# Second block: the token's rms scale moves from the operand of projection and MLP to the units behind them

## The chip, the cores and the metric

One core of one Trainium2 chip. The metric is the device time of one execution in microseconds, the median of the runs. One further execution was taken with the hardware profiler; the trace is from that one.

## The reference, cut to what matters

Two blocks one after the other on x, 256 tokens of 2048 numbers: an RWKV block with a modulated norm and a convolutional FFN (`first_block`), then the block that the change is about. `rmsnorm` divides each token by its root mean square and multiplies each feature by a weight.

```python
def rmsnorm(x, gain):
    xf = x.astype(jnp.float32)
    y = xf * lax.rsqrt(jnp.mean(xf * xf, axis=-1, keepdims=True) + EPS)
    return (y * gain.astype(jnp.float32)).astype(x.dtype)
...
        h = rmsnorm(x, mix_pre_gain[layer])
        proj = jnp.einsum('bsd,de->bse', h, w_in[layer])
        q_a, k_a, v_a, q_r, f_r, i_r, g_r = jnp.split(proj, SPLITS, axis=-1)
        attn = sliding_window_attention(q_a, k_a, v_a, attn_sinks[layer])
        attn = rmsnorm(attn, attn_out_gain[layer])
        rnn = hgrn2_chunkwise(q_r, f_r, i_r, g_r, lb_all[layer], rnn_norm_gain[layer])
        mixed = jnp.einsum('bse,ed->bsd', jnp.concatenate([attn, rnn], axis=-1), w_out[layer])
        x = x + rmsnorm(mixed, mix_post_gain[layer])
        h = rmsnorm(x, mlp_pre_gain[layer])
        u = jax.nn.relu(jnp.einsum('bsd,df->bsf', h, w_up[layer]))
        y = jnp.einsum('bsf,fd->bsd', u * u, w_down[layer])
        x = x + rmsnorm(y, mlp_post_gain[layer])
```

## The kernel before, in words

Every product is fp32 in three passes: each operand is split into a rounded half `hi` and a remainder `lo`, and hi x hi, hi x lo and lo x hi are added up in a PSUM bank. Weights come by DMA in pieces of 128 x 1024 (`wdma`), and `wsplit` splits them (L183 on ScalarE, L184 on VectorE) into three rotating buffers ahead of their use. The kernel fixes the order of the instructions itself: each engine's queue is the order in which the code issues them.

The stages follow each other: RWKV mixer, its FFN (`ffn`), second block's mixer (`mix`), MLP (`mlp`). `feat` and `feat_p` make a unit: 128 output features of all 256 tokens, 48 matmuls of 256 columns with the operand `hl` (features on partitions, hi and lo). A unit's result is evacuated from its bank some matmuls into the next unit (`deferred`, `flush`). The mixer has 42 units (`mix_evac`), and between their matmuls `mpump` issues the steps of three streams: attention heads and two alternating HGRN heads, due after so many slots. The MLP has 64 units (`ev`, L1813 and L1814).

A stage ends in a token-major product (`tok_all`, or `mix_out` and what follows it): eight banks `acc[tb, cb]`, tokens 0 to 127 (tb 0) or 128 to 255 (tb 1) by 512 columns. `tail` holds back the last weight pieces, so that tb 0 is finished first and then tb 1 in 12 steps, with the end of tb 0 issued between them. In `tail`:

- `col`: the sum of squares of a column block (ScalarE, L325) and its product z with the gain row G (VectorE, L372);
- `row`: the token's first rsqrt (sum L376, Ln L298, Exp L299), then four additions x += z * r (L380), each followed on ScalarE by the squares of the new x;
- `diag`: from the new squares the second rsqrt, multiplied onto the identity: a diagonal matrix `dg` (L391, L393);
- `xp`: 16 matmuls of x against `dg` (L403) turn the tokens' rows into features and scale each token at once; `prep_evac` multiplies each by its norm weight (L337, ScalarE, into `hb`), and `hilo` makes the two halves from `hb` (L285, L288, VectorE). `_attn_out` uses the same `prep_evac` in the middle of the mixer (L319).

`hook` splits weight pieces of the next stage at fixed steps. Two tails feed the second block and have no shift: that at the end of `ffn` (called from `tok_all`, steps of 3 pieces by 4 column blocks) and that at the end of `mix` (6 pieces by 2 column blocks). The tail of the RWKV mixer has a shift, that of the MLP has no next stage.

Of the kernel before, what the change touches and what calls it, by code (L numbers as in the profile page):

```python
# [19 lines left out]
D = 2048  # L20
# [77 lines left out]
class Kern:  # L98
# [228 lines left out]
    def prep_evac(self, wk, tb, hl, gain, shift):  # L327

        nc = self.nc
        t0 = slice(tb * 128, tb * 128 + 128)  # L330

        def evac(j, pt):
            h = wk.tile([128, 4, 128], F32, tag="hb", bufs=2, name="hb")
            for i in range(4):
                kc = j * 4 + i
                if shift is None:
                    nc.scalar.activation(out=h[:, i, :], in_=pt[:, i, :], func=AF.Copy, scale=gain(kc))  # L337
                else:
                    nc.scalar.activation(out=h[:, i, :], in_=pt[:, i, :], func=AF.Identity, scale=gain(kc),
                                         bias=shift(kc))  # L340
            self.hilo(hl[:, 0, j * 4:j * 4 + 4, t0], hl[:, 1, j * 4:j * 4 + 4, t0], h[:], True)
        return evac
# [13 lines left out]
    def tail(self, wk, acc, mm, cbs, G, z, gain, shift, banks, hook, hl=None):  # L356
# [4 lines left out]
        last = gain is None  # L361
        if not last and hl is None:
# [11 lines left out]
        def row(tb):  # L374
# [3 lines left out]
            for cb in range(4):  # L378
                w = slice(cb * 512, cb * 512 + 512)
                nc.vector.scalar_tensor_tensor(out=xt[:, tb, w], in0=z(tb, cb), scalar=r, in1=xt[:, tb, w],  # L380
                                               op0=ALU.mult, op1=ALU.add)
                if last:
                    nc.sync.dma_start(out=self.A["out"][tb * 128:tb * 128 + 128, w], in_=xt[:, tb, w])
                else:
                    self.ssq_(wk, xt[:, tb, w], ss[tb][:, 4 + cb:5 + cb])

        def diag(tb):
            if last:
                return
# [5 lines left out]
        def xp(tb):  # L395
            if last:
                return
            evac = self.prep_evac(wk, tb, hl, gain, shift)
            for j in range(4):
                pt = self.bank(banks[tb][j], (128, 4, 128), "xp")  # L400
                for i in range(4):
                    o = (j * 4 + i) * 128
                    nc.tensor.matmul(pt[:, i, :], lhsT=xt[:, tb, o:o + 128], rhs=dg[tb][:], start=True, stop=True)  # L403
                evac(j, pt)
                yield
# [8 lines left out]
        row(0)  # L414
        steps = [(cb, n) for cb in cbs for n in range(self.ntail)]
        x0 = xp(0)
        g = None
        for k, (cb, n) in enumerate(steps):
# [5 lines left out]
            if k == 2:  # L424
# [120 lines left out]
    def run(self):  # L545
# [69 lines left out]
        if "rwkv" not in ph:  # L615
            self.xt = self.rp.tile([128, 2, D], F32, tag="r", name="xt")
            nc.sync.dma_start(out=self.xt[:], in_=A["x"].rearrange("(b p) d -> p b d", p=128))
            nc.scalar.preload_act_table_set("natural_log_exp_and_others")
            with tc.tile_pool(name="pre", bufs=1) as wk:
                gain, shift = None, None  # L620
                if "ffn" in ph:
                    sc = self.scratch()
                    for _ in self.ada_sums(self.aunits, sc[:, 0:1024], [sc[:, 1024:2048], sc[:, 2048:3072]]):
                        pass
                    self.ada_cols()
                    gain, shift = self.gain_ffn()
                elif "mix" in ph:
                    gain = lambda kc: self.v("mixpre", kc)
                else:
# [1276 lines left out]
```

## Time and profile before

| what | value |
|---|---|
| median of 3 runs | 2756.57 us (2750.27 to 2757.24) |
| profiled execution | 2759.31 us, its span 2757.5 us |
| TensorE (PE) busy | 2608.1 us, 95% |
| VectorE (DVE) busy | 1775.8 us, 64% |
| ScalarE (ACT) busy | 1346.5 us, 49% |
| mean granted TensorE clock | 0.977 |
| mixer of the second block | about 1599 to 2029 us of the span |
| MLP | from 2029 us |

The span runs from the first to the last instruction of the trace; the time holds 1.8 us more around it. A granted clock of 1 is 2.4 GHz, 0.5 is 1.2 GHz. Matmuls are pipelined, so that the durations of neighbours overlap.

### The profile page before, as it was taken

Reading aid. Unit: us, or ns where it says so; the run is one execution under the profiler, and the core shown is the slowest. Engines: PE = TensorE matmul, PEld = TensorE weight load, DVE = VectorE, ACT = ScalarE, POOL = GpSimd, SP = SyncE. Lnnn points to the kernel's source line nnn. Section 1 sums busy time; section 2 is a strip of 40 time slices with the busy share of each in tenths; the row PEclk is TensorE's granted clock in tenths of the full one; section 3 lists DMA queues with packets and bytes.
Section 4 is the critical chain, followed back from the end, with each engine's and each line's share of the span. In section 5 each row is a group of like instructions: output and inputs, shape, how many; then the busy total and the mean of one; then the engine's idle time right before and its main releaser. Section 6 shows DMA issues by size and latency. Waiting matters only on the chain.

```text
span 2757.5 us, 47818 instructions
## 1 busy us (share of the span) xinstructions
PE 2608.1 (95%) x19345; PEld 2377.1 (86%) x19345; DVE 1775.8 (64%) x2845; ACT 1346.5 (49%) x2206; POOL 61.6 (2%) x101
## 2 busy tenths in 40 slices
PE   6997999998879999999999989999989999999998
PEld 5997788886559999999888789998789999988887
DVE  5977888887567786666555556665554444555555
ACT  3245565664355444444444555655454444444444
POOL 0000111110000000000000000000000000000000
PEclk8999999999889999999999999999999999999999
DMA  8946555556656775555555544443535555556555
GB/s 326 389 145 200 191 191 185 192 182 205 223 193 240 271 268 187 183 183 184 176 194 194 176 155 145 139 139 122 192 131 184 183 183 183 183 191 194 195 192 159
DMA packets 151516, 534.13 MB, mean 194 GB/s; under 512 B 21376, under 2 KB 21760, under 8 KB 150272
## 3 DMA queue, kind: packets, MB, share of 16 engines
q1 hardware_dynamic: 146640, 515.36, 55.7%
q0 software_dynamic: 4368, 13.64, 1.9%
q8 instruction: 151, 2.47, 0.4%
q10 hardware_dynamic: 288, 2.10, 0.2%
q14 instruction: 69, 0.57, 0.1%
HBM read 524.73 MB, written 6.29 MB: 193 GB/s over the span
## 4 chain that ended last, share of the span: by engine, by line
PE 82%; DVE 6%; ACT 6%; DMA 5%; issue 2%; SPq 0%; DVEq 0%; ACTq 0%; POOLq 0%
PE ta L353 7%; PE ta L354 7%; PE ta L352 7%; PE f L276 6%; PE f L274 6%; PE f L275 6%; PE u L276 4%; PE u L275 4%; PE u L274 4%; PE m L1043 3%; PE m L1044 3%; PE m L1045 3%; DMA scratch<-in_adat 2%; PE r L776 2%; DVE spl L184 1%
## 5 line engine op out<-in xcount | busy, mean ns | idle before, releaser
L184 DVE TENSOR_TENSOR spl<-raw,spl 128x1024 fp32r<-128x1024 f32 x748 | 913.1, 1221 | 778.0 <-ACT spl L183 773.6
L183 ACT CAST spl<-raw 128x1024 fp32r<-128x1024 f32 x748 | 782.0, 1046 | 856.8 <-PE ta L354 307.2
L276 PE MATMUL f<-yhl,spl 128*128 128x256 f32 x1376 | 389.5, 283 | 0.4 <-DVE spl L184 0.4
L274 PE MATMUL f<-yhl,spl 128*128 128x256 f32 x1376 | 389.8, 283 | 0.0
L275 PE MATMUL f<-yhl,spl 128*128 128x256 f32 x1376 | 389.4, 283 | 0.0
L352 PE MATMUL ta<-spl,shl 128*128 128x512 f32 x832 | 324.6, 390 | 3.4 <-ACT shl L287 3.4
L353 PE MATMUL ta<-spl,shl 128*128 128x512 f32 x832 | 324.5, 390 | 1.5 <-DVE spl L184 1.5
L354 PE MATMUL ta<-spl,shl 128*128 128x512 f32 x832 | 324.4, 390 | 0.0
L274 PE MATMUL u<-hl,spl 128*128 128x256 f32 x1024 | 289.9, 283 | 0.0
L276 PE MATMUL u<-hl,spl 128*128 128x256 f32 x1024 | 289.8, 283 | 0.0
L275 PE MATMUL u<-hl,spl 128*128 128x256 f32 x1024 | 289.8, 283 | 0.0
L276 PEld LDWEIGHTS f<-yhl,spl 128*128 128x128 f32 x1376 | 264.2, 192 | 0.6 <-DVE spl L184 0.6
L275 PEld LDWEIGHTS f<-yhl,spl 128*128 128x128 f32 x1376 | 264.2, 192 | 0.0
L274 PEld LDWEIGHTS f<-yhl,spl 128*128 128x128 f32 x1376 | 264.2, 192 | 0.0
L1043 PE MATMUL m<-hl,spl 128*128 128x256 f32 x672 | 199.6, 297 | 0.0
L274 PEld LDWEIGHTS u<-hl,spl 128*128 128x128 f32 x1024 | 196.6, 192 | 0.0
L275 PEld LDWEIGHTS u<-hl,spl 128*128 128x128 f32 x1024 | 196.6, 192 | 0.0
L276 PEld LDWEIGHTS u<-hl,spl 128*128 128x128 f32 x1024 | 196.6, 192 | 0.0
L1044 PE MATMUL m<-hl,spl 128*128 128x256 f32 x672 | 189.9, 283 | 0.0
L1045 PE MATMUL m<-hl,spl 128*128 128x256 f32 x672 | 189.8, 282 | 0.0
L352 PEld LDWEIGHTS ta<-spl,shl 128*128 128x128 f32 x832 | 156.6, 188 | 36.6 <-ACT shl L287 3.8
L353 PEld LDWEIGHTS ta<-spl,shl 128*128 128x128 f32 x832 | 156.6, 188 | 34.5 <-DVE spl L184 2.1
(422 smaller groups left out, 4809.8 us busy)
## 6 DMA issues: line engine op xcount, KB each, us to landing
raw<-in_ffn_in SPq DMA_DIRECT2D x172, 512.0 KB, 4.7
raw<-in_w_up SPq DMA_DIRECT2D x128, 512.0 KB, 3.7
raw<-in_w_down SPq DMA_DIRECT2D x128, 512.0 KB, 4.0
raw<-in_ffn_out SPq DMA_DIRECT2D x86, 512.0 KB, 3.8
raw<-in_w_in SPq DMA_DIRECT2D x84, 512.0 KB, 3.7
raw<-in_w_rkv SPq DMA_DIRECT2D x76, 512.0 KB, 4.5
scratch<-in_adat SPq DMA_DIRECT2D x66, 512.0 KB, 5.9
ada<-in_ada SPq DMA_DIRECT2D x64, 512.0 KB, 6.7
```

What stands on the lines that cost most here:

```text
L183: self.nc.scalar.copy(out=hi[:, :n], in_=t[:, :n])
L184: self.nc.vector.tensor_tensor(out=lo[:, :n], in0=t[:, :n], in1=hi[:, :n].bitcast(F32), op=ALU.subtract)
L274: nc.tensor.matmul(out, lhsT=hi[:, w], rhs=xhl[:, 0, kc, :], start=(kc == 0), stop=False)
L275: nc.tensor.matmul(out, lhsT=hi[:, w], rhs=xhl[:, 1, kc, :], start=False, stop=False)
L276: nc.tensor.matmul(out, lhsT=lo[:, w], rhs=xhl[:, 0, kc, :], start=False, stop=(kc == KD - 1))
L352: nc.tensor.matmul(o, lhsT=shl[0][:, t0], rhs=hi[:, w], start=first, stop=False)
L353: nc.tensor.matmul(o, lhsT=shl[0][:, t0], rhs=lo[:, w], start=False, stop=False)
L354: nc.tensor.matmul(o, lhsT=shl[1][:, t0], rhs=hi[:, w], start=False, stop=last)
L776: nc.tensor.matmul(out, lhsT=wd[:, w], rhs=xt[:, g % 2, max(0, min(3, ft - 9)), kc % 2, :], start=False, stop=e)
L1043: nc.tensor.matmul(out, lhsT=hi[:, w], rhs=xhl[:, 0, kc, :], start=(kc == 0), stop=False)
L1044: nc.tensor.matmul(out, lhsT=hi[:, w], rhs=xhl[:, 1, kc, :], start=False, stop=False)
L1045: nc.tensor.matmul(out, lhsT=lo[:, w], rhs=xhl[:, 0, kc, :], start=False, stop=(kc == KD - 1))
```

## The change

For a tail without a shift (`raw`), x itself is turned, not x times its rms scale: the transposes need only the addition of their block. The token's scale is computed afterwards; two matmuls of a matrix of ones with the two diagonals spread it over all partitions, and `token_scale` copies it to SBUF (`rb`, 128 x 256). Each unit's result is multiplied by `rb` when it is evacuated. `prep_evac` without a shift makes `hi` straight from the bank on ScalarE and `lo` from the bank and `hi` on VectorE, column block by column block; that holds for `_attn_out` too. A path of the program for runs without the RWKV stage is removed; it isn't used here.

```diff
@@ prep_evac
         def evac(j, pt):
+            if shift is None:
+                for i in range(4):
+                    kc = j * 4 + i
+                    hi, lo = hl[:, 0, kc, t0], hl[:, 1, kc, t0]
+                    nc.scalar.activation(out=hi, in_=pt[:, i, :], func=AF.Copy, scale=gain(kc))
+                    nc.vector.scalar_tensor_tensor(out=lo, in0=pt[:, i, :], scalar=gain(kc), in1=hi.bitcast(F32),
+                                                   op0=ALU.mult, op1=ALU.subtract)
+                return
             h = wk.tile([128, 4, 128], F32, tag="hb", bufs=2, name="hb")
             for i in range(4):
                 kc = j * 4 + i
-                if shift is None:
-                    nc.scalar.activation(out=h[:, i, :], in_=pt[:, i, :], func=AF.Copy, scale=gain(kc))
-                else:
...
@@ tail
         last = gain is None
+        raw = not last and shift is None
...
-        def row(tb):
+        def rms(tb):
             r = rs[tb][:, 0:1]
             nc.vector.tensor_reduce(out=r, in_=ss[tb][:, 0:4], axis=AX.X, op=ALU.add)
             self.rsqrt_(r, r, 1.0 / D, self.eps, False)
...
+        def add(tb, cb):
...
+        def square(tb, cb):
+            w = slice(cb * 512, cb * 512 + 512)
+            self.ssq_(wk, xt[:, tb, w], ss[tb][:, 4 + cb:5 + cb])
...
+        def turn(tb, j):
+
+            pt = self.bank(banks[tb][j], (128, 4, 128), "xp")
+            for i in range(4):
+                o = (j * 4 + i) * 128
+                if raw:
+                    nc.tensor.transpose(pt[:, i, :], xt[:, tb, o:o + 128], self.c("ident"))
+                else:
                     nc.tensor.matmul(pt[:, i, :], lhsT=xt[:, tb, o:o + 128], rhs=dg[tb][:], start=True, stop=True)
...
-        row(0)
+        rms(0)
+        for cb in range(4):
+            add(0, cb)
+            if not raw and not last:
+                square(0, cb)
         steps = [(cb, n) for cb in cbs for n in range(self.ntail)]
-        x0 = xp(0)
+        x0 = []
+        if raw:
+            for j in range(4):
+                x0 += [lambda j=j: evac[0](j, turn(0, j)), lambda j=j: square(0, j)]
+            x0.append(lambda: diag(0))
+        elif not last:
+            x0 = [lambda j=j: evac[0](j, turn(0, j)) for j in range(4)]
+        first = 3 if raw else len(steps) - 4
...
-            if k == 2:
+            if k == 2 and not raw and not last:
                 diag(0)
             if n == self.ntail - 1:
                 col(1, cb)
             hook(k)
-            if k >= len(steps) - 4:
-                next(x0, None)
-        row(1)
-        diag(1)
-        hook(-1)
-        for _ in xp(1):
-            pass
+            if k >= first and x0:
+                x0.pop(0)()
+        while x0:
+            x0.pop(0)()
+        rms(1)
+        if raw:
+            for j in range(4):
+                add(1, j)
+                evac[1](j, turn(1, j))
+            for j in range(4):
+                square(1, j)
+            diag(1)
+            self.rp_ = self.bank(rbank, (128, 2, 128), "rb")
+            for tb in range(2):
+                nc.tensor.matmul(self.rp_[:, tb, :], lhsT=self.c("ones"), rhs=dg[tb][:], start=True, stop=True)
+            hook(-1)
+        else:
...
+    def token_scale(self, pool):
+
+        self.rb = pool.tile([128, S], F32, name="rb")
+        self.nc.scalar.copy(out=self.rb[:], in_=self.rp_[:].rearrange("p a b -> p (a b)"))
...
@@ mix (mlp has the same with its pool)
+            self.deferred.append(lambda: self.token_scale(wk))
...
@@ mix_evac
+        def scaled(tag, bufs=1, by=1.0):
+
+            t = self.M([128, S], tag, bufs)
+            nc.vector.scalar_tensor_tensor(out=t, in0=p[:], scalar=by, in1=self.rb[:], op0=ALU.mult, op1=ALU.mult)
+            return t
...
         elif i == 9:
-            v = self.M([128, S], "va")
-            nc.scalar.copy(out=v, in_=p[:])
-            self.va = v
+            self.va = scaled("va")
...
-            q = self.M([128, S], "qa", 4)
-            nc.scalar.copy(out=q, in_=p[:])
-            self.mq["a"].append(self._attn(i, q))
+            self.mq["a"].append(self._attn(i, scaled("qa", 4)))
...
+            if w == 2:
+                d[w] = scaled("h2", 2)
+                self.mq[f"h{h % 2}"].append(self._hgrn(h, d))
+                return
+            x = scaled("hx", 2, 0.5)
+            t = d[w] = self.M([128, S], f"h{w}", 2)
+            nc.scalar.activation(out=t, in_=x, func=AF.Tanh)
...
@@ mlp
             def ev(p, i):
-                nc.scalar.activation(out=u[:, i, :], in_=p[:], func=AF.Relu)
-                nc.vector.tensor_tensor(out=u[:, i, :], in0=u[:, i, :], in1=u[:, i, :], op=ALU.mult)
+                nc.vector.scalar_tensor_tensor(out=u[:, i, :], in0=p[:], scalar=0.0, in1=self.rb[:], op0=ALU.max,
+                                               op1=ALU.mult)
+                nc.scalar.activation(out=u[:, i, :], in_=u[:, i, :], func=AF.Square)
```

## Rows read from the trace of the kernel before

**Rows 1.** The page: chain that ended last, and one of the costliest groups.

```profile
PE 82%; DVE 6%; ACT 6%; DMA 5%; issue 2%; SPq 0%; DVEq 0%; ACTq 0%; POOLq 0%
...
L183 ACT CAST spl<-raw 128x1024 fp32r<-128x1024 f32 x748 | 782.0, 1046 | 856.8 <-PE ta L354 307.2
```

**Rows 2.** Waits of TensorE over the span: us in total, times, longest.

```profile
PE xp L403 <- DVE dg L393: 35.7, 6, 10.7
```

**Rows 3.** Timeline of VectorE, mix tail: start us, us, engine, line, operation.

```profile
2004.52 2.74 DVE L380 SCALAR_TENSOR_TENSOR xt<-z,ers,xt 128x512 f32<-128x512 f32 x4 [0.60 <-ACT ers L299]
...
2018.81 2.74 DVE L380 SCALAR_TENSOR_TENSOR xt<-z,ers,xt 128x512 f32<-128x512 f32 x4 [0.60 <-ACT ers L299]
2022.61 0.16 DVE L391 TENSOR_REDUCE ers<-ess 128x1 f32<-128x4 f32 x1 [1.06 <-ACT junk L325]
2023.36 0.29 DVE L393 TENSOR_SCALAR dg<-cst,ers 128x128 f32<-128x128 f32 x1 [0.60 <-ACT ers L299]
```

**Rows 4.** Timeline of ScalarE, mix tail.

```profile
2004.28 0.20 ACT L299 ACTIVATE ers<-ers 128x1 f32<-128x1 f32 x1
...
2018.57 0.20 ACT L299 ACTIVATE ers<-ers 128x1 f32<-128x1 f32 x1
2019.59 0.63 ACT L325 ACTIVATE junk<-xt 128x512 f32<-128x512 f32 x1 [0.82 <-DVE xt L380]
...
2025.82 1.15 ACT L337 ACTIVATE hb<-xp,vec 128x128 f32<-128x128 f32 x4 [1.55 <-PE xp L403]
```

**Rows 5.** Timeline of TensorE, mix tail and first unit of the MLP.

```profile
2023.70 5.85 PE L403 MATMUL xp<-dg,xt 128*128 128x128 f32 x32 [8.37 <-DVE dg L393]
2029.31 0.36 PE L274 MATMUL u<-hl,spl 128*128 128x256 f32 x1
```

**Rows 6.** Timeline of the ffn tail, ScalarE and the mixer's first matmul.

```profile
1571.78 0.20 ACT L299 ACTIVATE ers<-ers 128x1 f32<-128x1 f32 x1
...
1587.37 0.20 ACT L299 ACTIVATE ers<-ers 128x1 f32<-128x1 f32 x1
...
1598.64 0.36 PE L1043 MATMUL m<-hl,spl 128*128 128x256 f32 x1
```

**Rows 7.** Timeline of ScalarE and VectorE, first columns of the ffn tail.

```profile
1567.55 0.19 ACT L325 ACTIVATION_READ_ACCUMULATOR junk<-ta 128x1 f32 x1
...
1567.78 2.13 DVE L372 TENSOR_TENSOR z<-ta,Gf 128x512 f32<-128x512 f32 x3 [0.78 <-ACT junk L325]
```

**Rows 8.** Line L1145: until when its engine sat idle (us, times).

```profile
  ACT Aa L1144: 7.5, 8
```

**Rows 9.** Groups by line and form on VectorE, 1600 to 1960: count | busy, mean ns.

```profile
L1767 DVE TENSOR_TENSOR QF<-QF,tot 128x128 f32<-128x128 f32 x48 | 13.8, 288 | 0.0
...
L1796 DVE SCALAR_TENSOR_TENSOR ho<-ho,vec,h 128x256 f32<-128x256 f32 x8 | 3.9, 485 | 0.3
```

**Rows 10.** Timeline of TensorE, four transposes of the first stage.

```profile
22.66 1.11 PE L739 MATMUL xp<-cst,x 128*128 128x128 f32 x4 [0.36 <-ACT x L734]
```

**Rows 11.** Windows: length, busy us (count) of PE, PEld, DVE, ACT, POOL; clock, DMA.

```profile
1592.50:1599.00 6.50, 6.50 (x35) 6.50 (x36) 3.47 (x5) 3.77 (x13) 0.00 (x0) 0.59 0.25 83
...
2023.70:2029.30 5.60, 5.59 (x32) 5.60 (x33) 2.91 (x5) 3.40 (x12) 0.00 (x0) 0.62 0.29 97
...
1604.00:1910.00 306.00, 298.31 (x2491) 293.25 (x2490) 190.36 (x483) 177.42 (x358) 0.00 (x0) 0.99 0.44 142
...
2032.00:2400.00 368.00, 367.23 (x3056) 366.77 (x3055) 178.41 (x195) 152.72 (x195) 0.00 (x0) 1.00 0.56 182
```

**Rows 12.** Waits of TensorE, 1600 to 1960.

```profile
PE xp L319 <- DVE dg L313: 5.8, 2, 5.3
...
PE mi L1670 <- ACT qa L1624: 0.6, 3, 0.2
```

**Rows 13.** Timeline, one q of the attention: ScalarE and VectorE.

```profile
1641.34 0.37 ACT L1624 COPY qa<-m 128x256 f32<-128x256 f32 x1
...
1641.47 1.23 DVE L184 TENSOR_TENSOR spl<-raw,spl 128x1024 fp32r<-128x1024 f32 x1 [1.20 <-ACT spl L183]
```

More of the change, by code (lines that the diff above doesn't have):

```diff
@@ L377, in row @@
             self.rsqrt_(r, r, 1.0 / D, self.eps, False)
[L378 to L385, printed above, removed]
+        def add(tb, cb):
+            w = slice(cb * 512, cb * 512 + 512)
+            nc.vector.scalar_tensor_tensor(out=xt[:, tb, w], in0=z(tb, cb), scalar=rs[tb][:, 0:1], in1=xt[:, tb, w],
+                                           op0=ALU.mult, op1=ALU.add)
+            if last:
+                nc.sync.dma_start(out=self.A["out"][tb * 128:tb * 128 + 128, w], in_=xt[:, tb, w])
+        def square(tb, cb):
+            w = slice(cb * 512, cb * 512 + 512)
+            self.ssq_(wk, xt[:, tb, w], ss[tb][:, 4 + cb:5 + cb])
         def diag(tb):
-            if last:
-                return
             r = rs[tb][:, 1:2]
@@ L428, in tail @@
             hook(k)
-            if k >= len(steps) - 4:
-                next(x0, None)
-        row(1)
-        diag(1)
-        hook(-1)
-        for _ in xp(1):
-            pass
+            if k >= first and x0:
[15 more added lines that the diff above has]
+        else:
+            for cb in range(4):
+                add(1, cb)
+                if not last:
+                    square(1, cb)
+            if not last:
+                diag(1)
+            hook(-1)
+            if not last:
+                for j in range(4):
+                    evac[1](j, turn(1, j))
         if not last:
             self.hl = hl
+    def token_scale(self, pool):
+        self.rb = pool.tile([128, S], F32, name="rb")
+        self.nc.scalar.copy(out=self.rb[:], in_=self.rp_[:].rearrange("p a b -> p (a b)"))
     def ada_start(self, groups, new, ahead):
@@ L614, in run @@
         self.wgrow(self.ctx.enter_context(tc.tile_pool(name="w2", bufs=1)), 1, 0)
[L615 to L629, printed above, removed]
-                    gain = lambda kc: self.v("mlppre", kc)
-                self.hl = self.hp.tile([128, 2, KD, S], F32R, tag="hl", bufs=2, name="hl")
-                for tb in range(2):
-                    ss = wk.tile([128, 4], F32, tag="ess", bufs=2, name="ess")
-                    for cb in range(4):
-                        self.ssq_(wk, self.xt[:, tb, cb * 512:cb * 512 + 512], ss[:, cb:cb + 1])
-                    self.xpose(wk, tb, self.xt[:, tb, :], ss[:], D, [4, 5, 6, 7],
-                               self.prep_evac(wk, tb, self.hl, gain, shift))
         if "ffn" in ph:
@@ L1613, in mix_evac @@
                 for h in range(2):
-                    nc.scalar.copy(out=self.kd[g][h * 64:h * 64 + 64, :], in_=p[g * 64:g * 64 + 64, :])
+                    nc.scalar.copy(out=self.kd[g][h * 64:h * 64 + 64, :], in_=k[g * 64:g * 64 + 64, :])
         elif i == 9:
-            v = self.M([128, S], "va")
-            nc.scalar.copy(out=v, in_=p[:])
-            self.va = v
+            self.va = scaled("va")
             self.mq["a"].append(self._avt())
@@ L1646, in mix_evac @@
             else:
-                t = d[w] = self.M([128, S], "h2", 2)
-                nc.scalar.copy(out=t, in_=p[:])
-                self.mq[f"h{h % 2}"].append(self._hgrn(h, d))
+                nc.vector.scalar_tensor_tensor(out=t, in0=t, scalar=1.0, in1=x, op0=ALU.add, op1=ALU.mult)
     def _avt(self):
```

33 lines of the change are left out of this document (9 added, 24 removed).

## The prediction

> **What bounds the kernel now.** The page's chain of work that ended last comes first: 82% of it is TensorE [rows 1]. So an edit pays or costs where it makes TensorE wait, and the list of waits says where that is. Its longest entry is six waits for the diagonal matrix that the tails build (L393), 35.7 us in all [rows 2]. There are two waits in each of three tails: at the end of the first block's mixer, of its FFN (the "ffn tail") and of the second block's mixer (the "mix tail"). The change rewrites the last two of these.
>
> The timeline shows what fills such a wait. In the mix tail the tokens 128 to 255 (tb 1) get their first rsqrt at 2018.57 + 0.20 = 2018.77 [rows 4]. Four additions to x follow, one straight behind the other [rows 3], with four squares on ScalarE, which start at 2019.59 [rows 4]. Then come sum, Ln, Exp and diagonal, from 2022.61 to 2023.65 [rows 3]; so a square takes (2022.61 - 2019.59) / 4 = 0.755. Only then do 32 transposing matmul instructions start, and the first matmul of the MLP starts at 2029.31 [rows 5]. From the rsqrt to there it is **10.5 us**. The same stretch of the ffn tail goes from 1587.57 to 1598.64, **11.1 us** [rows 6]. The stretch ahead of it, from the rsqrt of tb 0 to that of tb 1, is 14.3 us in the mix tail (2004.48 to 2018.77) [rows 4] and 15.6 us in the ffn tail (1571.98 to 1587.57) [rows 6]. In that one TensorE multiplies tb 1, and ScalarE and VectorE prepare tb 0.
>
> In these stretches each engine takes its instructions in the program's order. I see nothing that overtakes, and the argument rests on it.
>
> **The change part by part.**
>
> *One wait leaves.* The transposes of tb 1 no longer wait for squares, second rsqrt and diagonal. If that were all, about 4 us would be saved in each tail (2019.55, the end of the first addition, to 2023.65).
>
> *The evacuation of a block is split finer, and its halves share a bank.* Before: four ScalarE copies into `hb` (1.15 us, [rows 4]), then two VectorE instructions that read only SBUF, while ScalarE goes on with the next block. After: for each of 4 columns kc, ScalarE writes `hi` from the bank, and VectorE makes `lo` from the same bank and from `hi`. `lo` has to wait for its `hi`. Whether the next `hi` has to wait for this `lo` decides half of the result. The trace shows that two engines don't read one bank together: in `col` the product z reads the same bank as the square and doesn't need its result, but starts at 1567.78, after the accumulator read that began at 1567.55 and took 0.19 [rows 7]. L1145 reads other columns of a bank than L1144 and shares no data with it, and still waited for it eight times, 7.5 us [rows 8]. Both show VectorE behind ScalarE; the other direction doesn't occur. I take it that the order holds both ways. The Trainium skill ("PSUM — Partial Sum Buffer", section "PSUM bank collisions raise a hardware error") says that two engines on one bank and quadrant at once is an error, reads against reads included, so that software must order them. By the rows the order is certain one way, by the page both ways; if it is one way only, the sum is that of the second rival.
>
> So a column costs hi + lo + two handoffs, in series. hi: 0.37 (the four of 1.15 us overlap; one alone takes 0.37, as the copy L1624 of 256 columns does, [rows 13]). lo: a VectorE instruction with two tensors over 128 columns, between 0.29 (two tensors, no scalar) and 0.485 (the same operation over 256 columns) [rows 9]; from 256 to 512 columns this form grows by 0.26 (an addition takes 0.745: four in 2.74, each starting 0.08 before the last one ends, [rows 3]), so a quarter of 512 gives 0.35, which I take. A handoff is 0.03 to 0.04 (1567.74 to 1567.78, [rows 7]). A column is **0.78 us**, a block of four **3.1 us**.
>
> *Tokens 0 to 127 (mix tail).* ScalarE's queue, from the rsqrt at 2004.48: the weight split at step 2, with its VectorE half behind the four additions (4.52 + 2.74 = 7.26 [rows 3], plus 1.2 [rows 13]), holds the first `lo` until 2008.4. From there block 0 frees ScalarE at 2010.7; the second split's cast (1.0, [rows 1]), square (0.75) and the column square of tb 1 (0.75) reach 2013.2; block 1 with a z in VectorE's queue takes 3.0, to 2016.1; then twice square + block to its last `hi` (0.75 + 2.7) to 2023.0; square and column square to 2024.5; z 0.7; the diagonal of tb 0 (1.0) and the first rsqrt of tb 1 (0.65) to **2026.8**, against 2018.8: +8.0. In the ffn tail a column square comes every third step and the splits stand at steps 5 and 6: the first `lo` runs at 1575.3, behind additions and a z, and block 0 frees ScalarE at 1577.6; square, column square and cast 2.5, then block 1 behind the split's VectorE half to 1583.6; cast and square 1.7, block 2 to 1588.1; column square and square 1.5, block 3 to 1592.3; square and column square 1.5, z 0.7, diagonal 1.0, rsqrt 0.65: 1596.2 against 1587.6, +8.6. TensorE has long finished tb 1 by then, so nothing hides this.
>
> *Tokens 128 to 255.* `add(1, j)` stands in VectorE's queue behind the four `lo` of block j-1, so the additions don't run ahead any more. A block: addition 0.745, start 0.05, four transposes 1.11 (the slow ones of the start, [rows 10]; two matmul instructions each would take 1.7, and at full clock it is 0.6), start 0.035, four columns 3.1, less 0.08 by which VectorE's next starts before the last ends: 4.95 us, four of them 19.8. The squares come behind the last `hi` on ScalarE: -0.4 + 3.05. Sum to diagonal 1.1. Then two `ones` matmuls, four instructions at the slow spacing (5.85 us for 32 at mixed clock, 0.21 at the slow level) and their start, 0.9. They stand **ahead of the units' matmuls in TensorE's queue**, so the second rsqrt, which the change takes off the transposes, is still waited for before the next stage, only later. 19.8 - 0.4 + 3.05 + 1.1 + 0.9 = 24.4 us, against 10.5 and 11.1: **+13.9 and +13.3**.
>
> *The clock.* Before, the 32 transposing matmuls ran at a granted 0.62 and 0.59 [rows 11]: 0.76 of 5.6 us and 0.82 of 6.5 us at 1.2 GHz, 4.3 and 5.3 us. That dense work brought the clock back, and the units started at 2.4 GHz. Now TensorE has four short groups in some 20 us; I expect the units' first matmuls at 1.2 GHz for as long, which loses half of it: +2.1 and +2.7. If the transposes keep the clock up it is 0.
>
> *The mixer's units.* Each of 42 gets a VectorE instruction of about 0.48 us (256 columns) where ScalarE read the bank; it stands behind the VectorE half of a weight split. TensorE mostly needs the result much later, but not for q: it waited three times about 0.2 us for ScalarE's copy [rows 12]. There the split runs from 1641.47 to 1642.70, and q would come at 1643.1 instead of 1641.71 [rows 13]: +1.35, three times, and 0.8 for a fourth with little slack: 4.8. The transposes of v follow four slots behind their evacuation: about 1.5 over eight. The attention's output goes through the same evacuation; its second block adds 1.7 to the ScalarE chain at whose end TensorE already waits 5.3 us for L313 [rows 12]. **+8** together; 2 if the slots absorb all but q, 16 if each unit makes its stream late.
>
> *At nothing.* The MLP's units change engines (VectorE from the bank, ScalarE squares). Between 2032 and 2400 both are under half busy [rows 11] and a weight half is split 3 us early; without that cover it is 0.5 us a unit, 32 us. `token_scale`, one copy of 0.37, runs behind the units' first matmuls. Tails with a shift or without a next stage keep their order.
>
> **Sum:** ffn tail 8.6 + 13.3 + 2.7 = 24.6, mix tail 8.0 + 13.9 + 2.1 = 24.0, units 8: **+57 us**. The profiled execution took 2759.3 (span 2757.5), 2.7 above the median, so it would be 2816 and the median **2813**.
>
> **Rivals.**
>
> *Faster: the queues don't bind.* If the additions ran on as now and the `ones` matmuls came behind the first units, the units would follow the rsqrt by one addition and 16 transposes: 0.75 + 16 x 0.21 = 4.1 us, 6.4 and 7.0 less than now; with up to 4.8 for the clock and no units' waits that is -9, 2748. It decides if `add(1, 1)` starts before the `lo` of block 0. The longest wait of the list speaks for it, the strict order in every stretch I read against it. 0.06.
>
> *No order from VectorE's read to ScalarE's next.* Then tb 0 fits its present 14 to 16 us, and a block of tb 1 is 0.745 + 0.05 + 1.11 + 0.035 + 0.4 + 4 x 0.27 - 0.08 = 3.35; 24.4 becomes 18.0: +7.5 and +6.9, with 4.8 for the clock and 6 for the units +25: 2782. 0.08.
>
> *The units become the bound.* The 42 evacuations behind splits make the streams of the heads late, and TensorE waits at most of them; priced at 1.2 for 20 of them instead of 8 in all: +73, 2829. VectorE's share of 62% in the mixer (190 of 306 us, [rows 11]) leaves room, so 0.09.
>
> **How the numbers follow.** The forecast has 0.77; its own range, with `lo` from 0.29 to 0.42 (64 columns in series: -4 to +4.5), the clock from 0 to 4.8 and units from 2 to 14, is 2798 to 2824. The range 2785 to 2828 leaves out the faster case, most of the unordered one and the end of the last. A change under 0.3% (8 us) can hardly be told from none here; no case lies there, 0.02. Faster 0.06, slower 0.92.
>
> **What will show it.** In the tails: `hi` and `lo` taking turns at about 0.78 us; `add(1, j)` 4.9 us apart; a TensorE wait for the diagonal just ahead of two `ones` matmuls, some 22 us later after the rsqrt of tb 0 than now; the first units at 1.2 GHz. In the mixer: waits of L1670 for a VectorE q of over 1 us. I am wrong if `hi` runs on without `lo`, if the additions stay together, or if the units overtake the `ones`.

## The result

The changed kernel took **2821.36 us** (median of 4, 2817.76 to 2826.96), the kernel before on the same chip 2754.62 (2750.27 to 2757.24). The ratio is 1.0248, with a 95% interval from 1.0235 to 1.0261. That is 66.7 us more, 8.4 above the predicted 2813 and inside the predicted range.

A table of stages says where they are. A stage is cut at the first and last matmul that its tile's name shows in the trace, here for the profiled executions (span 2757.5 and 2825.2):

| stage, us | before | changed | difference |
|---|---|---|---|
| start of the FFN to its last matmul | 743.6 | 741.7 | -1.9 |
| gap to the mixer's first unit (ffn tail) | 16.7 | 39.1 | **+22.4** |
| the mixer's 42 units | 313.9 | 336.9 | **+23.0** |
| its output product | 101.9 | 100.4 | -1.5 |
| gap to the MLP's first unit (mix tail) | 14.9 | 37.2 | **+22.3** |
| the MLP's 64 units | 368.9 | 370.0 | +1.1 |
| the rest behind them | 359.4 | 359.7 | +0.4 |

The FFN also began 1.8 us later, ahead of anything that the change touches. The total is 67.6. The two gaps are near what the prediction said. The mixer's units are not. (A gap starts at TensorE's last matmul of the stage ahead. That matmul now ends earlier, the -1.9 and -1.5 of the table, so a gap grows by some 1.5 us more than the stretches from rsqrt to rsqrt and on to the first unit, by which the prediction counted.)

**The ffn tail.** This is the timeline of ScalarE, then of VectorE and of TensorE, in the changed kernel (the stretch of [rows 6]). L337 writes `hi`, L338 `lo`, L387 is the addition to x:

```profile
1573.28 0.20 ACT L299 ACTIVATE ers<-ers 128x1 f32<-128x1 f32 x1
...
1596.65 0.20 ACT L299 ACTIVATE ers<-ers 128x1 f32<-128x1 f32 x1
1598.85 0.37 ACT L337 ACTIVATE hl<-xp,vec 128x128 fp32r<-128x128 f32 x1 [1.99 <-PE xp L408]
1599.64 0.37 ACT L337 ACTIVATE hl<-xp,vec 128x128 fp32r<-128x128 f32 x1 [0.42 <-DVE hl L338]
1600.42 0.37 ACT L337 ACTIVATE hl<-xp,vec 128x128 fp32r<-128x128 f32 x1 [0.42 <-DVE hl L338]
```

```profile
1596.89 0.75 DVE L387 SCALAR_TENSOR_TENSOR xt<-z,ers,xt 128x512 f32<-128x512 f32 x1 [0.60 <-ACT ers L299]
1599.25 0.35 DVE L338 SCALAR_TENSOR_TENSOR hl<-xp,vec,hl 128x128 fp32r<-128x128 f32 x1 [1.61 <-ACT hl L337]
1600.04 0.35 DVE L338 SCALAR_TENSOR_TENSOR hl<-xp,vec,hl 128x128 fp32r<-128x128 f32 x1 [0.43 <-ACT hl L337]
...
1601.88 0.74 DVE L387 SCALAR_TENSOR_TENSOR xt<-z,ers,xt 128x512 f32<-128x512 f32 x1
```

```profile
1597.70 1.11 PE L408 MATMUL xp<-cst,xt 128*128 128x128 f32 x4 [15.85 <-DVE xt L387]
1602.68 1.11 PE L408 MATMUL xp<-cst,xt 128*128 128x128 f32 x4 [3.87 <-DVE xt L387]
...
1620.52 0.80 PE L461 MATMUL rb<-dg,cst 128*128 128x128 f32 x2 [6.34 <-DVE dg L400]
1620.96 0.56 PE L1063 MATMUL m<-hl,spl 128*128 128x256 f32 x1
```

The reader is to see three things. The bracket behind each `hi` names VectorE's `lo` as what ended 0.42 us of idle time, and behind each `lo` the `hi`: the two take turns, 0.787 us a column. The additions are 4.98 us apart, where the kernel before had them straight behind each other [rows 3]. And the first unit (L1063) stands behind the `ones` matmuls (L461), which waited 6.34 us for the diagonal.

From the rsqrt of tb 0 to that of tb 1 there are now 23.4 us (15.6 before [rows 6]), and from there to the first unit 24.1 (11.1). In the mix tail the rsqrts end at 2049.89 and 2071.35 and the first unit starts at 2095.46: 21.5 and 24.1, against 14.3 and 10.5 [rows 4, 5].

**The mixer.** The waits of TensorE in its stretch of units (us in total, times, longest) answer to [rows 12]:

```profile
PE xp L319 <- DVE dg L313: 8.9, 2, 6.9
...
PE mi L1781 <- DVE KB L1790: 5.0, 4, 2.1
PE mi L1691 <- DVE qa L1635: 4.9, 3, 1.7
PE mi L1759 <- DVE h L1635: 1.4, 3, 0.6
```

The three waits for q have grown from 0.2 to some 1.6 us each, as forecast. The wait at L1781, the product of a head's scan, was 0.2 us in all in the kernel before, and its growth wasn't forecast. Its place is read on three engines. Timeline of ScalarE in the kernel before, then of ScalarE, of VectorE and of TensorE in the changed kernel:

```profile
1723.76 0.38 ACT L1638 ACTIVATE h<-m 128x256 f32<-128x256 f32 x1
...
1727.62 1.03 ACT L183 CAST spl<-raw 128x1024 fp32r<-128x1024 f32 x1
```

```profile
1753.41 0.42 ACT L1665 ACTIVATE h<-hx 128x256 f32<-128x256 f32 x1 [3.09 <-DVE hx L1635]
1753.85 1.28 ACT L291 ACT_TABLE_LOAD   x1
...
1757.04 1.03 ACT L183 CAST spl<-raw 128x1024 fp32r<-128x1024 f32 x1
```

```profile
1751.50 1.22 DVE L184 TENSOR_TENSOR spl<-raw,spl 128x1024 fp32r<-128x1024 f32 x1
1752.63 0.42 DVE L1768 TENSOR_TENSOR att<-mi,cst 128x256 f32<-128x256 f32 x1
1752.96 0.41 DVE L1635 SCALAR_TENSOR_TENSOR hx<-m,rb 128x256 f32<-128x256 f32 x1
...
1758.10 1.23 DVE L184 TENSOR_TENSOR spl<-raw,spl 128x1024 fp32r<-128x1024 f32 x1 [0.58 <-ACT spl L183]
...
1759.71 0.28 DVE L1790 TENSOR_TENSOR KB<-KB,h 128x128 f32<-128x128 f32 x1
```

```profile
1760.14 1.08 PE L1781 MATMUL mi<-QF,KB 128*128 128x64 f32 x4 [1.96 <-DVE KB L1790]
```

Before the change ScalarE's tanh read the bank itself. Now it waits 3.09 us for VectorE's scaled copy `hx`, which stands behind a weight split. Behind the tanh in ScalarE's queue come a table load and at last the next weight half's cast (L183, 1757.04); VectorE waits for that cast, and what TensorE needs (L1790) stands behind the split. The unit in question began at 1729.76 in the kernel before, 2.1 us behind the start of that cast; in the changed kernel it began at 1756.22, 0.8 us ahead of it. The cast is thus 3.0 us later against TensorE, as much as the tanh waited. A loss of clock follows. These are windows of the changed kernel, the first the whole stretch of units, the last two the stretches at and after that wait:

```profile
1620.96:1958.00 337.04, 314.81 (x2557) 308.40 (x2557) 211.62 (x548) 172.83 (x330) 0.00 (x0) 0.97 0.41 132
...
1756.90:1760.00 3.10, 1.28 (x11) 1.08 (x9) 2.23 (x8) 2.24 (x8) 0.00 (x0) 1.00 0.00 0
1760.00:1763.30 3.30, 3.16 (x15) 3.19 (x16) 2.23 (x7) 1.78 (x3) 0.00 (x0) 0.51 0.48 161
```

TensorE was busy 1.28 of 3.10 us, and in the window after that it was granted 0.51, its lower level of 1.2 GHz. The unit there took 11.35 us, against 7.63 in the kernel before.

The whole list of waits in this stretch, without the `ones` ahead of it, grew from 7.6 to 22.2 us, by 14.6. The first unit has 1.1 of the stage's 23.0 us, so some 7.3 us are not waits. Behind the first unit the granted clock is 0.97 over 330 us, and was 0.99 over 308 us: an estimate from these is 6.8 us. By this estimate about a third of what the mixer lost is clock that fell behind its waits.

### The profile page after: what moved, and what is told of

Its sections match the earlier page's. It is cut to its first block, busy times and chain, and to the rows that moved or that the text cites. A ratio compares the mean times of both kernels' runs of the same rounds, so it can differ in the third digit from the quotient of the medians.

```text
span 2825.2 us, 47858 instructions
## 1 busy us (share of the span) xinstructions
PE 2618.6 (93%) x19289; PEld 2382.5 (84%) x19289; DVE 1796.7 (64%) x2927; ACT 1346.5 (48%) x2175; POOL 61.5 (2%) x101
## 5 line engine op out<-in xcount | busy, mean ns | idle before, releaser
L183 ACT CAST spl<-raw 128x1024 fp32r<-128x1024 f32 x748 | 781.0, 1045 | 740.5 <-PE ta L358 304.2
L356 PE MATMUL ta<-spl,shl 128*128 128x512 f32 x832 | 324.7, 390 | 3.9 <-ACT shl L287 3.9
L1063 PE MATMUL m<-hl,spl 128*128 128x256 f32 x672 | 202.3, 301 | 0.0
L1064 PE MATMUL m<-hl,spl 128*128 128x256 f32 x672 | 192.3, 286 | 0.0
L1065 PE MATMUL m<-hl,spl 128*128 128x256 f32 x672 | 192.0, 286 | 0.0
```

Source lines behind the costliest of these rows:

```text
L183: self.nc.scalar.copy(out=hi[:, :n], in_=t[:, :n])
L356: nc.tensor.matmul(o, lhsT=shl[0][:, t0], rhs=hi[:, w], start=first, stop=False)
L1063: nc.tensor.matmul(out, lhsT=hi[:, w], rhs=xhl[:, 0, kc, :], start=(kc == 0), stop=False)
L1064: nc.tensor.matmul(out, lhsT=hi[:, w], rhs=xhl[:, 1, kc, :], start=False, stop=False)
L1065: nc.tensor.matmul(out, lhsT=lo[:, w], rhs=xhl[:, 0, kc, :], start=False, stop=(kc == KD - 1))
```

## Experiments

All ran against the kernel before, experiments 1 to 4, 5 to 8 and 9 to 10 each on one chip, where the kernel before had medians of 2755.67, 2755.22 and 2752.43 us. The ratios are to these. The table has the measured times and four stages of the profiled executions, cut as above ("gaps" are the ffn tail and the mix tail):

| kernel | median us (runs) | ratio, 95% interval | gap ffn | mixer units | gap mix | MLP units |
|---|---|---|---|---|---|---|
| before | 2754.62 (4) | 1 | 16.7 | 313.9 | 14.9 | 368.9 |
| changed | 2821.36 (4) | 1.0248, 1.0235 to 1.0261 | 39.1 | 336.9 | 37.2 | 370.0 |
| 1 buffer | 2793.39 (4) | 1.0133, 1.0105 to 1.0160 | 26.5 | 332.9 | 24.8 | 370.8 |
| 2 late scale | 2813.39 (4) | 1.0213, 1.0192 to 1.0234 | 31.0 | 342.8 | 29.1 | 373.6 |
| 3 two banks | 2801.73 (4) | 1.0165, 1.0139 to 1.0191 | 30.8 | 339.6 | 28.9 | 370.3 |
| 4 no scaling | 2802.38 (4) | 1.0173, 1.0151 to 1.0196 | 39.0 | 320.0 | 37.1 | 370.0 |
| 5 evacuation first | 2807.95 (4) | 1.0186, 1.0171 to 1.0201 | 39.1 | 324.7 | 37.2 | 371.1 |
| 6 MLP alone | 2764.25 (6) | 1.0028, 1.0016 to 1.0040 | 16.5 | 313.9 | 24.8 | 370.6 |
| 7 MLP alone, late | 2747.55 (6) | 0.9970, 0.9956 to 0.9984 | 16.7 | 313.9 | 7.9 | 370.0 |
| 8 both, late | 2743.06 (9) | 0.9961, 0.9947 to 0.9975 | 9.8 | 322.4 | 8.2 | 369.8 |
| 9 additions first | 2754.62 (10) | 1.0009, 0.9997 to 1.0022 | 16.5 | 313.9 | 15.6 | 371.4 |
| 10 split first | 2757.07 (10) | 1.0013, 1.0003 to 1.0023 | 9.8 | 331.7 | 8.2 | 370.0 |

**1. The evacuation of before.**

```diff
         def evac(j, pt):
-            if shift is None:
-                for i in range(4):
-                    kc = j * 4 + i
-                    hi, lo = hl[:, 0, kc, t0], hl[:, 1, kc, t0]
-                    nc.scalar.activation(out=hi, in_=pt[:, i, :], func=AF.Copy, scale=gain(kc))
-                    nc.vector.scalar_tensor_tensor(out=lo, in0=pt[:, i, :], scalar=gain(kc), in1=hi.bitcast(F32),
-                                                   op0=ALU.mult, op1=ALU.subtract)
-                return
             h = wk.tile([128, 4, 128], F32, tag="hb", bufs=2, name="hb")
             for i in range(4):
                 kc = j * 4 + i
...
+                if shift is None:
+                    nc.scalar.activation(out=h[:, i, :], in_=pt[:, i, :], func=AF.Copy, scale=gain(kc))
...
             self.hilo(hl[:, 0, j * 4:j * 4 + 4, t0], hl[:, 1, j * 4:j * 4 + 4, t0], h[:], True)
```

> Edit: the changed kernel, with the evacuation of the kernel before in both tails and after the attention: four ScalarE copies of a block into an SBUF buffer, then one cast and one subtraction on VectorE. My theory (within one PSUM bank ScalarE's and VectorE's reads take turns both ways, 0.787 us a column): a tb1 block falls from 4.98 us to some 4.2 (addition 0.75, transposes to the first copy 0.9, copies 1.5, cast and subtraction 1.0, of which the last lie beside the next block), and the stretch of the tb0 blocks in the tail gives back its 7.8 us; 9 to 11 us a tail, 1 to 3 in the mixer, so 20 to 25 us less than the changed kernel, 2797 to 2801. Rival (the columns' order costs nothing, the queues' order of blocks and additions alone stretches the tails): within 4 us of the changed kernel, 2818 to 2825.

By the medians 28 us less than the changed kernel, more than the 20 to 25 expected: 12.6 and 12.4 in the tails, 4.1 in the mixer. VectorE's timeline in the ffn tail of this kernel shows the block:

```profile
1582.16 0.75 DVE L383 SCALAR_TENSOR_TENSOR xt<-z,ers,xt 128x512 f32<-128x512 f32 x1 [0.60 <-ACT ers L299]
1585.30 0.43 DVE L285 CAST hl<-hb 128x512 fp32r<-128x512 f32 x1 [2.38 <-ACT hb L337]
1585.76 0.69 DVE L288 TENSOR_TENSOR hl<-hb,hl 128x512 fp32r<-128x512 f32 x1
1586.37 0.75 DVE L383 SCALAR_TENSOR_TENSOR xt<-z,ers,xt 128x512 f32<-128x512 f32 x1
```

An addition follows the last after 4.2 us, as expected, and the tb 0 stretch is 14.6 us in place of 23.4. The rival falls. The gap is still 10 us above the kernel before: the evacuation is somewhat over half of a tail's loss, and the additions between the blocks are in what is left.

**2. The scale off the path to the units.** `diag` now ends with the rsqrt, which stays in `sm`; `token_scale` is called with unit 0's evacuation.

```diff
+            hook(-1)
             for j in range(4):
                 square(1, j)
             diag(1)
-            self.rp_ = self.bank(rbank, (128, 2, 128), "rb")
-            for tb in range(2):
-                nc.tensor.matmul(self.rp_[:, tb, :], lhsT=self.c("ones"), rhs=dg[tb][:], start=True, stop=True)
-            hook(-1)
...
     def token_scale(self, pool):
         self.rb = pool.tile([128, S], F32, name="rb")
+        self.rp_ = self.bank(self.rbank_, (128, 2, 128), "rb")
+        for tb in range(2):
+            d = self.rb[:, tb * 128:tb * 128 + 128]
+            self.nc.vector.tensor_scalar(out=d, in0=self.c("ident"), scalar1=self.sm[:, 20 + tb:21 + tb], scalar2=None,
+                                         op0=ALU.mult)
+            self.nc.tensor.matmul(self.rp_[:, tb, :], lhsT=self.c("ones"), rhs=d, start=True, stop=True)
```

> Edit: the changed kernel, with the tokens' scale taken off the path to the units: the next weights' split goes ahead of the four squares of tb1, and diagonals, the two ones matmuls and the copy of the scale are issued with the first unit's evacuation. My theory (in the changed kernel the first unit stands in TensorE's queue behind the ones matmuls, which wait 6.3 us for squares, sums and Ln/Exp): the first unit of the mixer comes 1.1 us after the last block's transposes begin, at about 1614 in place of 1621, and so in the MLP; 7 us a tail, 14 in all, 2805 to 2810. Rival 1 (the units need the last block's low part anyway): they start at 1617, 4 us a tail, 2812 to 2815. Rival 2 (the scale is then late for the first evacuations and the units wait for their banks): no gain, 2819 to 2825.

The units started 8.1 us earlier in both tails, more than the 7 expected: the place of the `ones` matmuls is what held them. (The weight split ahead of the squares belongs to the same edit and wasn't tried alone.) But 9.5 us were given back in the units, 5.9 in the mixer and 3.6 in the MLP, and the total of 2813.39 missed the 2805 to 2810 expected. The mixer's second unit took 11.92 us, not 5.76. TensorE's timeline says why:

```profile
1617.68 1.19 PE L484 MATMUL rb<-rb,cst 128*128 128x128 f32 x4 [2.85 <-DVE rb L482]
```

The diagonals stood behind two weight splits in VectorE's queue. The wait is 2.85 of the 6.16 us; behind it the granted clock was 0.50 from 1617.6 to 1623.6. So rival 2's wait is there too, at a smaller price, and 2813 is a sum of both that only looks like rival 1.

**3. Two banks in turn for tb 1.**

```diff
-                add(1, j)
-                evac[1](j, turn(1, j))
+            for j in (0, 2):
+                add(1, j)
+                pa = turn(1, j)
+                add(1, j + 1)
+                pair(j, pa, turn(1, j + 1))
...
+        def pair(j, pa, pb):
+            for i in range(4):
+                two = [(pa, j * 4 + i), (pb, j * 4 + 4 + i)]
+                for pt, kc in two:
+                    nc.scalar.activation(out=hl[:, 0, kc, 128:256], in_=pt[:, i, :], func=AF.Copy, scale=gain(kc))
+                for pt, kc in two:
+                    nc.vector.scalar_tensor_tensor(out=hl[:, 1, kc, 128:256], in0=pt[:, i, :], scalar=gain(kc),
+                                                   in1=hl[:, 0, kc, 128:256].bitcast(F32), op0=ALU.mult,
+                                                   op1=ALU.subtract)
```

> Edit: the changed kernel, with the blocks of tb1 in pairs: two additions, the transposes into two banks, and the columns of the two banks in turn (high a, high b, low a, low b). My theory (the two engines take turns within a bank, and not otherwise): a pair of columns takes 2 x 0.37 us and not 2 x 0.787, four blocks of tb1 some 12 us and not 19.9; 8 us a tail, 16 in all, 2803 to 2808. Rival (each engine answers the other with some 0.4 us whatever the bank, since a low part waits for its high part's semaphore): a pair still takes 1.5 us, and only the paired additions gain, 1 to 2 us a tail, 2817 to 2820.

In ScalarE's timeline of this kernel two `hi` now take 0.79 us together, where one column had 0.787:

```profile
1594.06 0.62 ACT L417 ACTIVATE hl<-xp,vec 128x128 fp32r<-128x128 f32 x2 [0.49 <-PE xp L408]
1594.85 0.62 ACT L417 ACTIVATE hl<-xp,vec 128x128 fp32r<-128x128 f32 x2 [0.16 <-DVE hl L419]
```

```profile
1594.46 0.61 DVE L419 SCALAR_TENSOR_TENSOR hl<-xp,vec,hl 128x128 fp32r<-128x128 f32 x2 [0.50 <-ACT hl L417]
```

The gaps fell by 8.3 us each, as the theory had it; the total of 2801.73 is a little under the expected 2803. So it is the bank, and not a delay in every answer between the engines, that makes the columns take turns. Nor is it the tile `hl`, which both engines write: the `hi` of 1594.85 starts while VectorE's pair from 1594.46, whose second `lo` is of the other bank, runs until 1595.07.

**4. The mixer without the scale.** Its units are evacuated as before the change, and the scale of the mixer's operand is left out.

> Edit: the changed kernel, with the mixer's units evacuated as in the kernel before, by ScalarE and without the tokens' scale; this leaves out the scale of the mixer's operand, so its outputs are those of an operand that is not normed. My theory (the 23 us that the mixer's stage of units grew by come from the scaling on VectorE, behind which ScalarE's gates and casts and then TensorE wait): the stage falls from 337 us to 316 to 320, the total to 2800 to 2805. Rival (the stage grew by the evacuation of the attention's output and by the clock alone): it falls by 3 to 5 us, total 2816 to 2819.

The stage of units fell to 320.0 us, the total to 2802.4. So of its 23 us, 17 are the scaling's. Of the other 6.1, the first unit has 1.2 and the last four, in which the attention's output is evacuated column by column, 4.9. In experiment 1, with that evacuation through the buffer, these four took 4.8 us less than in the changed kernel.

**5. The evacuation ahead of the split.**

```diff
-    def feat_p(self, out, xhl, pump):
+    def feat_p(self, out, xhl, pump, early=False):
...
         for half in range(2):
+            if early and half == 0:
+                self.flush()
             hi, lo = self.wnext()
...
-                self.feat_p(p[:], hl, self.mpump)
+                self.feat_p(p[:], hl, self.mpump, True)
```

> Edit: the changed kernel, with each of the mixer's units evacuated ahead of the next unit's weight split in the queues, and not four weight blocks into that unit. My theory (the 17 us that the scaling on VectorE costs the mixer are a matter of order: the scaled copy stands behind a weight split of 1.2 us and the attention's operations, and the gates' tanh, the weights' casts and TensorE wait for it): the stage of units falls from 337 us by 8 to 15, the total to 2806 to 2813. Rival 1 (it is the work itself that VectorE and ScalarE cannot hide where a head's scan sits): within 3 us of the changed kernel, 2818 to 2824. Rival 2 (ahead of the split, the evacuation waits for the unit's last matmul and holds the split back): longer than the changed kernel.

The stage took 324.7 us: 12 of the 17 were the order. Waits of TensorE in it:

```profile
PE mi L1783 <- DVE KB L1792: 2.3, 2, 1.8
...
PE mi L1693 <- DVE qa L1637: 0.5, 3, 0.2
```

q costs what it did before, the scan half of what it did in the changed kernel. But that half is uneven. In the unit shown above the wait went from 1.96 to 1.76 us only: the scaled copy now stands behind the attention's operations on VectorE in place of the split, and ScalarE sits idle for 5.07 us ahead of the tanh until that copy comes. That unit took 9.61 us and not 11.35 mostly because no lower clock followed the wait. At the other scan the wait of 2.13 became 0.54 and 0.59. Without the unit shown above, the order is worth 10.5 us. Of the 4.7 that remain against experiment 4, the two scans have 3.8 and the first unit 1.1. The scans are where rival 1 put it, but its time is 10 us off; rival 2 falls.

**6. The change in the mix tail and the MLP alone**, with experiment 1's evacuation.

> Edit: the change made in the mixer's tail and the MLP alone, with the evacuation of the kernel before (buffer, cast, subtraction); the mixer and its operand are as in the kernel before. My theory (the parts add): against the kernel before only the second tail changes, by the 9.9 us that it showed with that evacuation in both tails, and the MLP's units by 1.1; 2766 to 2768 against 2756. Rival 1 (the first tail's delay moves the mixer's weights and with them the second tail): more than 4 us away from that. Rival 2 (with the operand's columns no longer alternating, the second tail alone is free): within 3 us of the kernel before.

2764.25, 9.0 above the kernel before on this chip (2755.22), some 2 under the forecast. Gap mix is 24.8, the same as in experiment 1, so the parts add, and both rivals fall.

**7. The same with additions first and a late scale.** `token_scale` now builds the two diagonals alone; `token_rows` has the `ones` matmuls and the copy, and runs with unit 1's evacuation.

```diff
             for j in range(4):
                 add(1, j)
+            for j in range(4):
                 evac[1](j, turn(1, j))
+            hook(-1)
             for j in range(4):
                 square(1, j)
...
-            self.deferred.append(lambda: self.token_scale(up))
+            held = []
+            self.token_scale(up)
...
+                if i == 1:
+                    self.deferred += [self.token_rows] + held
+                (held if i == 0 else self.deferred).append(lambda p=p, i=i: ev(p, i))
```

> Edit: as the one before (change in the mixer's tail and the MLP alone, with the evacuation of the kernel before), and tb1's four additions ahead of its blocks, the weights' split ahead of its squares, and the scale built at the MLP's start and used from the second unit's evacuations on. My theory (the raw operand can free the units from the second rsqrt only when additions and squares are off the blocks' path): the units begin some 4.2 us after the rsqrt of tb1 (four additions of 0.75, transposes 1.1), where the kernel before has some 11, and the tb0 stretch is 1.5 us shorter; 8 to 9 us less, of which the MLP's units give back 1 to 2; 2747 to 2750 against 2756. Rival 1 (the units start early and then wait for the low parts, VectorE's 1.15 us a block, or run at the lower clock): 2753 to 2757. Rival 2 (the scale comes too late and TensorE waits for it as it did with the scale in the first unit's evacuation): 2755 to 2760.

2747.55: **faster than the kernel before by 0.30%**, at the expected place; both rivals' times lie above it. Timeline of ScalarE and TensorE in the mix tail:

```profile
2011.38 0.20 ACT L299 ACTIVATE ers<-ers 128x1 f32<-128x1 f32 x1
```

```profile
2012.42 3.34 PE L405 MATMUL xp<-cst,xt 128*128 128x128 f32 x16 [4.85 <-DVE xt L383]
2015.52 0.36 PE L274 MATMUL u<-hl,spl 128*128 128x256 f32 x1
```

The 16 transposes run in one piece, and the units begin 3.9 us behind the rsqrt (4.2 expected, 10.5 in [rows 4, 5]).

**8. Both tails so, and the mixer's evacuation ahead of the split.**

> Edit: the whole change with the evacuation of the kernel before, tb1's additions ahead of its blocks, the split ahead of its squares, the late scale, and the mixer's evacuation ahead of the weight split. My theory: two tails of 8 to 9 us less each, against a mixer that is 6 to 19 us longer than in the kernel before (6 without any scaling, 19 with it behind the split); 2745 to 2758 against 2756, and no better than the change in the MLP alone. Rival (the mixer hides its scaling once the order is right): 2735 to 2742.

2743.06, the lowest of all: 2 us under the expected range, and above the rival's. Against experiment 7, the first gap is 6.9 us shorter and the mixer's units are 8.6 longer, which would leave it behind. But 4.1 us less lie ahead of the ffn tail's gap and 2.1 in the output product. Two of the 4.1 are the change's: before and changed kernel differ by 1.9 there too. The other two are the clock. TensorE's first matmul of the FFN's token-major product waits 2.64 us in either kernel, and these are the windows of experiments 7 and 8 that begin 0.8 us after this wait:

```profile
1335.71:1339.71 4.00, 4.00 (x12) 3.15 (x11) 1.50 (x2) 0.93 (x2) 0.00 (x0) 0.57 0.21 63
1335.45:1339.45 4.00, 4.00 (x19) 3.32 (x18) 2.17 (x3) 2.08 (x3) 0.00 (x0) 1.00 0.18 56
```

The same wait is followed by a granted 0.57 in one and by 1.00 in the other; in the profiled executions of 5, 8 and 9 the clock stayed up. Of the 2.1, the wait for the last head's operand (L287) has 0.8: it is 0.54 us in experiments 5 and 8, and 1.3 in all other kernels. The intervals of the two ratios overlap: which kernel is better stays open.

**9. Additions first, everything else as in experiment 6.**

> Edit: the change in the mixer's tail and the MLP alone, with the evacuation of the kernel before, and one thing more: tb1's four additions stand ahead of its blocks. Squares, scale and the ones matmuls keep the change's places. My theory: additions 3.0, then four blocks of VectorE's 1.15, squares on ScalarE from 6.4 after the rsqrt, diagonal at 10.6, units at 11.5; the change with additions between the blocks had 20.3 there, so 8.8 us less than it (2764) and level with the kernel before (2754 to 2758): moving the additions is half of the gain of the late version, the scale off TensorE's queue the other half. Rival (the additions didn't matter, the scale's place alone did): 2760 to 2765.

2754.62, level with the kernel before; the gap fell by 9.2 us. Additions ahead of the blocks give the first half of experiment 7's gain, the scale off TensorE's queue together with the split ahead of the squares (15.6 to 7.9) the other.

**10. Experiment 8 with the evacuation behind the split again.**

> Edit: the late version of the whole change, with the mixer's evacuation back at its place four weight blocks into the next unit, behind the split. My theory (the split ahead of the scaled copy costs the mixer 12 us, as it did in the changed kernel): the stage of units goes from 322 to 334 us, the total from 2743 to 2753 to 2757, level with the kernel before. Rival (the 12 us hung on the late start of the units in the changed kernel): within 4 us of 2743.

The units' stage is 331.7 in place of 322.4, somewhat under the 334 expected; the total is 14 us up by the medians, of which 2.1 is the clock in the FFN and 1.4 the output product. The order's price is 9.3 us here and 12.2 in experiment 5. The difference is the unit shown above, where the clock fell in the changed kernel and in experiment 8, and not in 5 and 10. Without that unit the price is 10.7 here and 10.5 there: it doesn't hang on when the units start.

## Why the prediction was right, and where it was not

- **The order within a bank** was the step on which half the sum stood, and it held in both directions: 0.787 us a column against 0.78, each engine's idle time ended by the other's read. Experiments 1 and 3 show it by taking it away in two ways. This agrees with the Trainium skill ("PSUM — Partial Sum Buffer", section "PSUM bank collisions raise a hardware error"), by which reads of two engines on one bank need an order in either direction; the rows of before had shown only one. The rival without it would have been at 2782.
- **The tb 0 stretch**: +7.8 and +7.2 measured, +8.6 and +8.0 predicted.
- **From the rsqrt of tb 1 to the units**: +13.0 and +13.6, predicted +13.3 and +13.9. The block (4.98 against 4.95), the queue of squares and the wait at the `ones` were as worked out. Experiment 2 shows that wait is the one that counts at the end.
- **The clock**: the first unit of each stage took 1.1 us longer (6.96 and 6.94 against 5.84), predicted 2.7 and 2.1. The units did start at 1.2 GHz, by an estimate from the mean of 0.82 (shown at the end) for some 2.5 of their first 6.96 us, and not for as long as the transposes had.
- **At nothing**: the MLP's units grew by 1.1, all of it the first unit. Right.
- **The mixer's units: the term that was mis-sized.** +8 was predicted, with 2 to 16 as bounds; measured 23.0, of which 1.1 is the clock of the first unit counted above, so 21.9. By units: the three behind q +4.3 (predicted 1.35 each: right); six others +3.4 (v 1.5 and a fourth q 0.8 predicted); the last four, with the attention's output, +6.6 (predicted 1.7; 4.9 of it stays in experiment 4, so it is the column evacuation); and two units of the scans +7.5, for which the prediction had nothing. Nor had it anything for a clock that falls inside the stage, about a third of the whole. The step that failed is "TensorE mostly needs the result much later, but not for q". It asked when TensorE needs the stream, and not what stands behind ScalarE's tanh: the weights' casts. The list of waits of the kernel before couldn't show this, since no wait of note stood there.

Tails, mixer and clock make 21.9 + 21.9 + 21.9 = 65.7; predicted 24.6 + 24.0 + 8. The tails were 4.8 us too dear and the mixer 13.9 too cheap. That the total came within 8.4 us is in part luck: the errors have opposite signs, and the mixer's term lies outside its own bounds, near the 24 of the third rival. It didn't come about as that rival said, by 20 units at 1.2 us each: 15 of the 41 units behind the first grew, and the two scans and the last four units have some 14 of the 21.9.

The idea of the change was not wrong. Its one saved wait is worth 6.9 us in the mix tail (experiment 7; the faster rival had 6.4), once what was put in its place is cleared away: 12.4 us by the shared bank, 9.2 by additions between blocks, 7.7 by the `ones` ahead of the units, with the split's place. They are measured in this order, one on top of the other; gap mix went 37.2, 24.8, 15.6, 7.9.

## What to carry to other kernels

When an operation moves to another engine, ask what stands behind its reader in that reader's queue, and not only when the last consumer needs it: here a tanh that waited 3 us for its scaled copy made a weight cast behind it late, with it a split on VectorE, and with that TensorE. Where two engines take the halves of one result from one bank, alternate between two banks, or let one read and the other work from SBUF. And a wait is gone only when no instruction that needs the same value stands ahead of the critical work in the same queue.

## What was not expected of the hardware

In the changed kernel a wait of TensorE of 1.96 us in the mixer was followed by a lower clock: after it was busy for 1.28 of 3.10 us, it was granted 0.51 in the window behind, so the unit lost 3.7 us around that wait. But the same wait doesn't always cost this. In experiment 10 it is 1.96 us long too, in the same unit, and the windows at and after it read:

```profile
1721.06:1724.16 3.10, 1.28 (x11) 1.08 (x9) 2.23 (x8) 2.24 (x8) 0.00 (x0) 1.00 0.00 0
1724.16:1727.46 3.30, 3.16 (x27) 3.19 (x28) 2.23 (x7) 1.96 (x4) 0.00 (x0) 1.00 0.46 159
```

The engines were busy for nearly the same times, the granted clock stayed at 1.00, and the unit lost 2.2 us, not 3.7. So single stages of two profiled executions can differ by 1.5 to 2 us by the clock alone, as in experiment 8's FFN. What decides it is not shown by these runs. Over the stage of the mixer's units the granted clock is 0.97; the same stage of experiment 5, with shorter waits, has 0.98. In the other direction, the first unit of the changed kernel's mixer, behind a tail of short groups of transposes, has a mean of 0.82, and the rest of its first third 1.00.

```profile
1620.96:1627.92 6.96, 6.96 (x50) 6.96 (x50) 3.63 (x11) 1.64 (x4) 0.00 (x0) 0.82 0.52 173
1627.92:1740.00 112.08, 109.49 (x917) 107.43 (x916) 71.87 (x169) 55.66 (x102) 0.00 (x0) 1.00 0.46 151
```
